# Loading the first quarter of w in two rounds through the same SBUF rows, and a different set of warm-up matmuls

## The chip, the cores and the metric

The kernel runs on one core of one Trainium2 chip. A core has a matrix engine (TensorE, PE in the profile, whose weight loads are listed apart as PEld), a vector engine (VectorE, DVE), a scalar engine (ScalarE, ACT), a general engine (GpSimd, POOL) and SyncE (SP), which only issues transfers here. SP and ACT issue loads whose type stays as it is (float32 to float32); POOL's loads convert float32 to bfloat16 on the way. The metric is the device time of one execution in microseconds. Before the change it is 904.03 us, the median of three runs (903.47 to 904.25).

## What is computed

x has 16 batches of 2048 time steps of 1024 values, w is 1024 by 1024, decay has one value for each of the 1024 output columns, all in float32. The reference is a matrix product followed by a running sum that decays:

```python
xw = x @ w
out[:, 0, :] = xw[:, 0, :]
for t in range(1, S):
    out[:, t, :] = decay[None, :] * out[:, t - 1, :] + xw[:, t, :]
```

## The kernel before

**The tiles.** Time is cut into chunks of 512 steps, 64 in all. For a chunk the kernel loads x as bfloat16 into a tile `xb`, turns it on DVE in 32 by 32 blocks into `xw` (the method `turn`, line 110), and copies it into `xt`, where the elements that lie in pairs are taken apart (the method `part`, line 119). The 1024 rows of w are the contraction. They are spread over the 128 partitions in four quads of 32 (q), and over 8 steps k; a step k = 2m + e has a row set m (0 to 3) and a parity e (0 or 1). A matmul (line 131) multiplies one step k of one block of 128 output columns n with up to 512 time steps, and eight of them add up in PSUM. Steps of parity 0 can read `xw` directly (argument `pairs`), those of parity 1 read `xt`. What follows the product (the scan along time on DVE, help from ACT and POOL, a turn back, the stores by SP) is not touched by the change.

**w.** The weights stay in SBUF as bfloat16 in `wsb`. They come in four quarters, named by a half of the columns h and a parity e. Quarter (0, 0) is loaded as float32 by SP and ACT, four loads of 256 KB (one for each quad, two on each engine), before anything else. The other three are loaded by POOL as bfloat16, four loads of 128 KB each. A quarter lies first in a staging area (`stage`, line 312), which borrows the room of output tiles, and is then copied into `wsb` by `settle` (line 324), one row set m at a time. For quarter (0, 0) that copy is also the cast from float32.

**The order.** Every instruction is pinned: each engine works off its own in the order in which the program writes them. For the start that order is a string, `agenda[-99]`, whose letters are functions of the table `deeds`, and whose numbers are their arguments:

- M0 to M3 load the halves of x's first two chunks, four loads of POOL each (one for each quad). The first chunk is cut into 320 and 192 time steps, the second into 256 and 256. U0 to U2 load w's quarters (0, 1), (1, 0) and (1, 1) by POOL.
- W and w settle one row set of w, W on DVE and w on ACT. Numbers 0 to 3 are quarter (0, 0), 4 to 7 quarter (0, 1).
- E turns one row set of one part of x on DVE. F (on DVE) and G (on ACT) do the copy into `xt`.
- K3 copies one value of x's quad 3 into a small tile `gate` (`spin_on`, line 355, on ACT), and then issues a matmul that uses `gate` as weights, so that TensorE stays in its place until x has come.
- R loads the decays by SP, D works on them.

Ahead of the agenda stand the loads of quarter (0, 0), three fills on DVE (`wide`, `seed`, `gate`), a copy on ACT from `wide` into `seed`, which brings ACT's table load with it, and `spin(5, seed, wide)`: five float32 matmuls of 512 columns, whose results are not used and whose weights `seed` wait for that copy. In the profile a float32 matmul appears as two records.

After the agenda TensorE starts the first chunk (line 653 on): for the first 320 time steps it takes the parity-0 steps k = 0, 2, 4, 6 with quarter (0, 0), four column blocks each, then k = 1, 3, 5, 7 with quarter (0, 1), and then the same for the other 192 time steps. The second chunk follows, in halves of 256.

Of the kernel before, what the change touches and what calls it, by code (L numbers as in the profile page):

```python
# [9 lines left out]
FP32 = mybir.dt.float32  # L10
BF16 = mybir.dt.bfloat16
# [3 lines left out]
def _ap(ap_obj: bass.AP, new_ap, extra_offset=0):  # L15
    return dataclasses.replace(
        ap_obj,
        ap=[list(p) for p in new_ap],
        offset=ap_obj.offset + extra_offset,
    )  # L20
# [5 lines left out]
def kernel(  # L26
# [26 lines left out]
    nc = tc.nc  # L53
    pin = tc.keep_in_program_order
    B, S, D = x.shape
    assert w.shape == (D, D)

    NQ = 4
    P = 32
    CQ = D // NQ  # L60
    K = CQ // P
    M = K // 2
# [3 lines left out]
    R = K // 2  # L66
    CH = D // 2
    CR = CH // NQ

    const = ctx.enter_context(tc.tile_pool(name="const", bufs=1))  # L70
# [9 lines left out]
    def quad(q):  # L80
        return slice(q * P, (q + 1) * P)
# [12 lines left out]
    def ot_tile(nj):  # L94
        return ring(sb, "ot", 4, [128, nj, CR])
# [14 lines left out]
    def turn(c, j0=0, j1=NJ, m0=0, m1=M):  # L110
        if c not in xw_of:
            xw_of[c] = ring(sb, "xw", 2, [128, M, NJ, P, 2], BF16)
        src = xb_of[c][:, j0:j1].rearrange("p j c -> p (j c)").bitcast(FP32)
        dst = xw_of[c].rearrange("p m j i e -> p (m j i e)").bitcast(FP32)
        pin(nc.vector.transpose(  # L115
            out=dst.rearrange("p (m j i) -> p j m i", m=M, i=P)[:, j0:j1, m0:m1],
            in_=src.rearrange("p (j m c) -> p j m c", m=M, c=P)[:, :, m0:m1]))
# [23 lines left out]
    class Tile:  # L141
# [45 lines left out]
        def copy(self):  # L187
            self.xs = sb.tile([128, 2 * TL], FP32, name=f"xs{self.lot % 3}")[:, 0:self.T]
            size = self.T // len(self.parts())
            for i, ps in enumerate(self.parts()):  # L190
                pin(nc.scalar.copy(out=self.xs[:, i * size:(i + 1) * size], in_=ps))  # L191
# [94 lines left out]
    class Outlet:  # L286
# [8 lines left out]
        def store(self, b, t0):  # L295
# [4 lines left out]
            for j in range(0, self.nj, nj):  # L300
# [8 lines left out]

    room = [ot_tile(2 * NJ).rearrange("p j c -> p (j c)") for _ in range(2)]  # L310
    size = M * CH
    stage = {(0, 0): room[0][:, 0:size],
             (0, 1): room[0][:, size:size * 3 // 2].bitcast(BF16),
             (1, 0): room[1][:, 0:size // 2].bitcast(BF16),
             (1, 1): room[1][:, size // 2:size].bitcast(BF16)}

    def load_w(queues, h, e):
        for i, q in enumerate((0, 2, 1, 3)):
            pin(queues[i % len(queues)].dma_start(  # L319
                out=stage[h, e][quad(q)].rearrange("p (m d) -> p m d", m=M),  # L320
                in_=_ap(w, [[2 * D, P], [2 * P * D, M], [1, CH]],
                        (q * CQ + e) * D + h * CH)))

    def settle(h, e, m, copy):
        src = stage[h, e][:, m * CH:(m + 1) * CH]
        pin(copy(out=wcols[:, 2 * m + e, h],  # L326
                 in_=src.rearrange("p (q r i) -> p q r i", q=NQ, r=R)))

    wide = const.tile([128, TL], FP32, name="wide")
    idle = wide[:, 0:TL // 2].bitcast(BF16)  # L330
    spare = ring(psp, "spare", 1, [128, TL])
    rows = const.tile([128, 2, P], FP32, name="rows")
    seed = const.tile([128, 128], FP32, name="seed")
    load_w((nc.sync, nc.scalar), 0, 0)
    pin(nc.vector.memset(wide, 0.0))
    pin(nc.vector.memset(seed, 0.0))
    pin(nc.scalar.copy(out=seed[:, 0:1], in_=wide[:, 0:1]))  # L337

    gate = const.tile([128, 128], BF16, name="gate")
    pin(nc.vector.memset(gate, 0.0))  # L340

    def spin(count, by, on):
        for _ in range(count):
            pin(nc.tensor.matmul(out=spare, lhsT=by, rhs=on, start=True, stop=True))  # L344

    spin(5, seed, wide)
    H = NJ // 2
    cuts = (((0, H + 2), (H + 2, NJ)), ((0, H), (H, NJ)))
    cols = const.tile([128, 2, P], FP32, name="cols")
# [8 lines left out]

    def load_part(i):
        load_w((nc.gpsimd,), *((0, 1), (1, 0), (1, 1))[i])  # L360

    def part_one(i, copy):
        part(i // 8, copy, i % 4, i % 4 + 1, *cuts[i // 8][i // 4 % 2])

    def settle_one(i, copy):
        settle(i // 8, i // 4 % 2, i % 4, copy)
# [119 lines left out]
    def turn_and_load(c):  # L486
# [16 lines left out]
        "w": lambda i: settle_one(i, nc.scalar.copy),  # L503
        "M": load_half,
        "U": load_part,
        "r": await_settled,
        "E": lambda i: turn(i // 8, *cuts[i // 8][i // 4 % 2], i % 4, i % 4 + 1),
        "F": lambda i: part_one(i, nc.vector.tensor_copy),
# [20 lines left out]
        "L": lambda i: load(*loads.pop(0)) if loads else None,  # L529
    }  # L530
    agenda = {
        -99: "M0 U0 M1 M2 M3 U1 U2 w0 W1 w2 W3 K3 E0 E1 G0 E2 G1 E3 F2 G3 W4 w5 W6 W7 E4 E5 G4 E6 G5 E7 F6 G7 R E8 E9 G8 E10 G9 E11 F10 G11 E12 L E13 G12 L E14 G13 E15 L F14 G15 D",
        0: "",
        1: "",
        2: "",
# [104 lines left out]
    for step, (g, n) in enumerate(slots):  # L640
# [11 lines left out]
        if step == 0:  # L652
# [9 lines left out]
            Q = cuts[1][0][1] * P  # L662
# [93 lines left out]
```

## Time and profile before

| what | value |
|---|---|
| median of three runs | 904.03 us (903.47 to 904.25) |
| the profiled execution's own time | 903.32 us |
| its span in the profile | 901.5 us |
| TensorE busy | 894.6 us, 99% |
| DVE, ACT, POOL busy | 825.8, 685.7, 656.8 us |
| moved by the transfers | 204.77 MB, mean 227 GB/s |
| first float32 matmul of the spins | 3.21 us |
| first settling of w | 7.04 us |
| x's first part turned from | 10.33 us |
| first matmul of the product | 10.90 us |

The times count from the start of the span. A line of the timeline gives the start, the duration, the engine, the line of the kernel, the operation, what it writes and reads, and in brackets how long the engine was idle just before it and what ended that. A line of the transfers' table gives a queue with its packets, megabytes and the share of 16 transfer engines' time; q0 is POOL's queue, q1 is SP's and q10 is ACT's. A line of the table of issues gives what is written and read, the issuing engine, the number of loads, the size of one and the median time from issue to landing.

### The profile page before, as it was taken

To read this page: it belongs to the slowest core of one execution; us is meant where nothing else is said; L and a number is where in the kernel's file an instruction comes from. 1 tells how busy PE (TensorE), PEld (TensorE's weight loads), DVE (VectorE), ACT (ScalarE), POOL (GpSimd) and SP (SyncE) were. 2 spreads that over 40 slices of the span, in tenths; PEclk is the share of its full clock that TensorE was granted. 3 is DMA by queue.
4 is the path that set the end of the run, shared out by engine and by line. 5 is a ranking of instruction groups with operands and counts; after the bars stand their busy time and mean duration, and the time that the engine had idled before them with its cause. 6 is when DMAs were issued, how large, how long until landed. Compare 5 with 4: busy or idle time off the path is not lost.

```text
span 901.5 us, 12309 instructions
## 1 busy us (share of the span) xinstructions
PE 894.6 (99%) x4211; PEld 412.8 (46%) x4211; DVE 825.8 (92%) x633; ACT 685.7 (76%) x957; POOL 656.8 (73%) x758
## 2 busy tenths in 40 slices
PE   8999999999999999999999999999999999999998
PEld 5544444444444444444444444444444444444444
DVE  4999989999999999999998999989999999999998
ACT  4888879877877877878778778777787787787743
POOL 7887778877767768677677687777777777776532
PEclk9999999999999999999999999999999999999999
DMA  9999999999999999999999999999999999999658
GB/s 189 192 211 244 244 205 215 215 230 240 248 237 264 242 254 242 256 253 246 220 245 218 228 241 211 239 223 228 236 228 223 229 235 226 230 219 219 187 135 239
DMA packets 403182, 204.77 MB, mean 227 GB/s; under 512 B 9392, under 2 KB 402096, under 8 KB 403120
## 3 DMA queue, kind: packets, MB, share of 16 engines
q0 software_dynamic: 137024, 68.70, 57.5%
q1 hardware_dynamic: 265808, 134.77, 57.1%
q8 instruction: 33, 0.54, 0.2%
q10 hardware_dynamic: 288, 0.52, 0.2%
q14 instruction: 29, 0.24, 0.1%
HBM read 138.42 MB, written 134.22 MB: 302 GB/s over the span
## 4 chain that ended last, share of the span: by engine, by line
PE 99%; ACT 0%; ACTq 0%; DVE 0%; DVEq 0%; issue 0%
PE ps L131 97%; PE spare L131 1%; PE spare L344 1%; ACT L337 0%; PE spare L412 0%; ACTq L319 0%; PE ps L412 0%; DVE h L440 0%; ACT seed L337 0%; DVEq L751 0%
## 5 line engine op out<-in xcount | busy, mean ns | idle before, releaser
L131 PE MATMUL ps<-xt,wsb 128*128 128x512 bf16 (+2 forms) x4040 | 865.9, 377 | 0.0
L131 PEld LDWEIGHTS <-wsb 128*128 128x128 bf16 x4184 | 408.3, 98 | 477.2 <-DVE wsb L326 0.3
L205 POOL TENSOR_TENSOR xs<-h,xs 128x512 f32<-128x512 f32 (+1 forms) x190 | 242.4, 1277 | 185.5 <-ACT h L171 84.4
L191 ACT COPY xs<-ps 128x1024 f32<-128x1024 f32 (+1 forms) x190 | 188.7, 994 | 153.4 <-PE ps L131 147.2
L278 DVE STREAM_TRANSPOSE ot<-so 128x1024 f32<-128x1024 f32 (+2 forms) x264 | 300.6, 1176 | 2.7 <-POOL so L266 2.0
L266 POOL TENSOR_TENSOR so<-h,xs 128x512 f32<-128x512 f32 (+1 forms) x189 | 240.6, 1274 | 38.4 <-ACT h L171 26.2
L123 ACT COPY xt<-xw 128x2048 bf16<-128x2048 bf16 (+3 forms) x136 | 242.4, 1788 | 5.8 <-DVE xw L115 5.8
L105 POOL DMA_DIRECT2D xb<-in_x_dram x264 | 173.8, 659 | 7.6 <-DMA xb<-in_x_dram 2.8
L171 ACT ACTIVATE h<-so,dec 128x512 f32<-128x512 f32 (+1 forms) x189 | 144.7, 766 | 26.6 <-DVE so L210 23.3
L115 DVE STREAM_TRANSPOSE xw<-xb 128x2048 f32<-128x2048 f32 (+3 forms) x78 | 147.2, 1899 | 6.1 <-DMA xb<-in_x_dram 6.1
L210 DVE TENSOR_TENSOR_SCAN so<-spare,keep,xs 128x512 f32<-128x512 f32 (+1 forms) x97 | 120.0, 1240 | 27.5 <-POOL xs L205 26.9
L210 DVE TENSOR_TENSOR_SCAN so<-spare,xs 128x512 f32<-128x512 f32 x93 | 113.3, 1220 | 25.9 <-POOL xs L205 22.6
L171 ACT ACTIVATE h<-ps,dec 128x512 f32<-128x512 f32 (+1 forms) x190 | 129.6, 683 | 0.0
L229 DVE TENSOR_TENSOR_SCAN so<-dec,ps 128x1024 f32<-128x1024 f32 x34 | 76.9, 2261 | 0.8 <-ACT h L171 0.6
L229 DVE TENSOR_TENSOR_SCAN so<-dec,keep,ps 128x1024 f32<-128x1024 f32 (+2 forms) x35 | 75.5, 2156 | 0.8 <-PE ps L131 0.8
L270 ACT COPY keep<-so 128x1 f32<-128x1 f32 x136 | 25.3, 188 | 9.3 <-DVE so L229 8.7
L201 ACT COPY so<-keep 128x1 f32<-128x1 f32 x97 | 18.3, 191 | 3.3 <-DVE ot L278 3.2
L199 POOL MEMSET so<- 128x1 f32 x93 | 10.6, 115 | 3.0 <-DVE ot L278 3.0
L131 PE MATMUL spare<-xt,wsb 128*128 128x512 bf16 (+3 forms) x60 | 12.6, 329 | 0.0
L131 PE MATMUL ps<-xw,wsb 128*128 128x256 bf16 (+3 forms) x72 | 12.2, 306 | 0.0
L344 PE MATMUL spare<-wide,seed 128*128 128x512 f32 x10 | 7.4, 915 | 3.2 <-ACT seed L337 3.2
L319 POOL DMA_DIRECT2D ot<-in_w_dram x12 | 6.5, 548 | 0.7 <-issue 0.3
(43 smaller groups left out, 37.6 us busy)
## 6 DMA issues: line engine op xcount, KB each, us to landing
out_dram<-ot SPq DMA_DIRECT2D x236, 512.0 KB, 8.9
xb<-in_x_dram POOLq DMA_DIRECT2D x248, 256.0 KB, 7.4
out_dram<-ot SPq DMA_DIRECT2D x56, 128.0 KB, 2.2
out_dram<-ot SPq DMA_DIRECT2D x8, 256.0 KB, 4.8
ot<-in_w_dram POOLq DMA_DIRECT2D x12, 128.0 KB, 5.8
xb<-in_x_dram POOLq DMA_DIRECT2D x8, 128.0 KB, 4.5
out_dram<-xb SPq DMA_DIRECT2D x3, 256.0 KB
xb<-in_x_dram POOLq DMA_DIRECT2D x4, 160.0 KB, 6.6
```

The lines of the kernel that those rows point to most:

```text
L105: pin(nc.gpsimd.dma_start(out=xb_of[c][quad(q), j0:j1], in_=_ap(x, [[D, P], [P * D, j1 - j0], [1, CQ]], (b * S + t0 + j0 * P) * D + q * CQ)))
L115: pin(nc.vector.transpose(out=dst.rearrange("p (m j i) -> p j m i", m=M, i=P)[:, j0:j1, m0:m1], in_=src.rearrange("p (j m c) -> p j m c", ...
L123: pin(copy(out=xt_of[c][:, m0:m1, :, j0 * P:j1 * P], in_=src))
L131: return pin(nc.tensor.matmul(out=ps[:, t0 % ps.shape[1]:][:, 0:t1 - t0], lhsT=lhs, rhs=rhs, start=(k == 0 and t0 == start), stop=(k == K ...
L171: pin(nc.scalar.activation(out=h[:, i * size:(i + 1) * size], in_=src, func=mybir.ActivationFunctionType.Copy, scale=dec[:, self.n:self.n ...
L191: pin(nc.scalar.copy(out=self.xs[:, i * size:(i + 1) * size], in_=ps))
L205: pin(nc.gpsimd.tensor_tensor(out=odds, in0=self.g, in1=odds, op=ALU.add))
L210: pin(nc.vector.tensor_tensor_scan(out=so[:, 3:T + 2:2], data0=squares[-1][:, n:n + 1].to_broadcast([128, T // 2]), data1=self.xs[:, 1:T:2 ...
L229: return pin(nc.vector.tensor_tensor_scan(out=so[:, t + 2:t + 2 + size], data0=dec[:, n:n + 1].to_broadcast([128, size]), data1=ps, initia ...
L266: pin(nc.gpsimd.tensor_tensor(out=self.so[:, 2:T + 2:2], in0=self.h, in1=self.xs[:, 0:T:2], op=ALU.add))
L270: pin(nc.scalar.copy(out=self.keep, in_=self.so[:, self.T + 1:self.T + 2]))
L278: pin(nc.vector.transpose(out=outlet.ot[:, :, c0:c0 + P], in_=self.so[:, 2 + t0:2 + t0 + nj * P].rearrange("p (i t) -> p i t", t=P)))
```

## The change

Quarter (0, 0) comes in two rounds, of row sets 0 and 1 and of row sets 2 and 3. Both go into the same rows of the staging area (`rounds`), so that the second round can be written only when both row sets of the first have been settled. Each round is four loads of 128 KB, two on SP and two on ACT; the second is the new deed Q. In the agenda, Q stands behind w0 and W1, and the settling of row sets 2 and 3 (w2 on ACT, W3 on DVE) moves behind gates and turns of x. There is one more gate, K2, for x's quad 2. The turns E0 to E3 stand ahead of the copies G0, G1, F2, G3, and w2 and W3 among them.

The spins become four float32 matmuls that read `wide` for the weights as well, and so wait for its fill and no longer for ACT's copy, and two bfloat16 matmuls with `gate`. `seed` shrinks to one column and loses its fill; ACT's copy into it stays.

```diff
-    stage = {(0, 0): room[0][:, 0:size],
-             (0, 1): room[0][:, size:size * 3 // 2].bitcast(BF16),
+    early = M // 2
+    rounds = room[0][:, 0:early * CH]
+    stage = {(0, 1): room[0][:, size:size * 3 // 2].bitcast(BF16),
...
-    def load_w(queues, h, e):
+    def staged(h, e, m0, m1):
+        if (h, e) == (0, 0):
+            return rounds[:, m0 % early * CH:][:, 0:(m1 - m0) * CH]
+        return stage[h, e][:, m0 * CH:m1 * CH]
+
+    def load_w(queues, h, e, m0=0, m1=M):
         for i, q in enumerate((0, 2, 1, 3)):
             pin(queues[i % len(queues)].dma_start(
-                out=stage[h, e][quad(q)].rearrange("p (m d) -> p m d", m=M),
-                in_=_ap(w, [[2 * D, P], [2 * P * D, M], [1, CH]],
-                        (q * CQ + e) * D + h * CH)))
+                out=staged(h, e, m0, m1)[quad(q)].rearrange("p (m d) -> p m d", m=m1 - m0),
+                in_=_ap(w, [[2 * D, P], [2 * P * D, m1 - m0], [1, CH]],
+                        (q * CQ + e + 2 * P * m0) * D + h * CH)))
 
     def settle(h, e, m, copy):
-        src = stage[h, e][:, m * CH:(m + 1) * CH]
         pin(copy(out=wcols[:, 2 * m + e, h],
-                 in_=src.rearrange("p (q r i) -> p q r i", q=NQ, r=R)))
+                 in_=staged(h, e, m, m + 1).rearrange("p (q r i) -> p q r i", q=NQ, r=R)))
...
-    seed = const.tile([128, 128], FP32, name="seed")
-    load_w((nc.sync, nc.scalar), 0, 0)
+    seed = const.tile([128, 1], FP32, name="seed")
+    load_w((nc.sync, nc.scalar), 0, 0, 0, early)
     pin(nc.vector.memset(wide, 0.0))
-    pin(nc.vector.memset(seed, 0.0))
-    pin(nc.scalar.copy(out=seed[:, 0:1], in_=wide[:, 0:1]))
+    pin(nc.scalar.copy(out=seed, in_=wide[:, 0:1]))
...
-    spin(5, seed, wide)
+    spin(4, wide[:, 0:128], wide)
+    spin(2, gate, idle)
...
+    def load_rest(i):
+        load_w((nc.sync, nc.scalar), 0, 0, early, M)
...
+        "Q": load_rest,
...
-        -99: "M0 U0 M1 M2 M3 U1 U2 w0 W1 w2 W3 K3 E0 E1 G0 E2 G1 E3 F2 G3 W4 w5 W6 W7 E4 E5 ...
+        -99: "M0 U0 M1 M2 M3 U1 U2 w0 W1 Q K2 K3 E0 E1 w2 E2 E3 W3 G0 G1 F2 G3 W4 w5 W6 W7 E4 E5 ...
```

## The prediction, made before the changed kernel was run

> **What bounds the kernel now.** I read the page's busy table and chain first, to see which engine sets the end.
>
> ```profile
> span 901.5 us, 12309 instructions
> PE 894.6 (99%) x4211; PEld 412.8 (46%) x4211; DVE 825.8 (92%) x633; ACT 685.7 (76%) x957; POOL 656.8 (73%) x758
> PE 99%; ACT 0%; ACTq 0%; DVE 0%; DVEq 0%; issue 0%
> ```
>
> TensorE is the chain. From its first real matmul at 10.90 us it has no idle time until the last microseconds, so whatever moves its first tile moves the end by as much. The change touches only the stretch before 20 us; I went through it in order of time.
>
> ```profile
> 3.21 7.42 PE L344 MATMUL spare<-wide,seed 128*128 128x512 f32 x10 [3.21 <-ACT seed L337]
> 7.04 1.14 ACT L326 CAST wsb<-ot 128x512 bf16<-128x512 f32 x2 [3.87 <-DMA ot<-in_w_dram]
> 7.07 0.76 DVE L326 CAST wsb<-ot 128x512 bf16<-128x512 f32 x2 [5.45 <-DMA ot<-in_w_dram]
> 10.29 0.19 ACT L356 COPY gate<-xb 32x1 bf16<-32x1 bf16 x1 [2.11 <-DMA xb<-in_x_dram]
> 10.33 1.69 DVE L115 STREAM_TRANSPOSE xw<-xb 128x320 f32<-128x320 f32 x4 [2.50 <-DMA xb<-in_x_dram]
> 10.88 1.98 ACT L123 COPY xt<-xw 128x640 bf16<-128x640 bf16 x3 [0.40 <-DVE xw L115]
> 12.92 0.62 ACT L326 COPY wsb<-ot 128x512 bf16<-128x512 bf16 x1
> 12.94 0.70 DVE L326 COPY wsb<-ot 128x512 bf16<-128x512 bf16 x3 [0.54 <-DMA ot<-in_w_dram]
> 15.00 1.16 DVE L115 STREAM_TRANSPOSE xw<-xb 128x192 f32<-128x192 f32 x4 [1.36 <-DMA xb<-in_x_dram]
> 17.71 1.42 DVE L115 STREAM_TRANSPOSE xw<-xb 128x256 f32<-128x256 f32 x4 [1.24 <-DMA xb<-in_x_dram]
> 20.42 1.42 DVE L115 STREAM_TRANSPOSE xw<-xb 128x256 f32<-128x256 f32 x4 [0.98 <-DMA xb<-in_x_dram]
> ```
>
> w's first quarter lies in SBUF at 7.0, the first part of x at 10.3, the second quarter (POOL's first w loads) at 12.9, the rest of x's first chunk at 15.0, the next chunk's halves at 17.7 and 20.4. TensorE turns to each at 10.90, 13.29, 15.48, 18.21 and 21.77. The first four come 0.3 to 0.6 us after the data, a transpose or copy and no more: TensorE and the transfers run level here.
>
> Last the transfers, in three windows: 0 to 5.4, 16.5 to 20.0 and 20.0 to 21.4 us.
>
> ```profile
> q1 hardware_dynamic: 275, 0.51, 41.5%
> q10 hardware_dynamic: 227, 0.43, 20.7%
> xb<-in_x_dram POOLq DMA_DIRECT2D x4, 160.0 KB, 6.6
> ot<-in_w_dram POOLq DMA_DIRECT2D x3, 128.0 KB, 7.2
> ```
>
> ```profile
> q0 software_dynamic: 1350, 0.68, 143.4%
> rows<-in_decay_dram SPq DMA_DIRECT2D x4, 1.0 KB
> ```
>
> ```profile
> q0 software_dynamic: 304, 0.28, 121.3%
> q1 hardware_dynamic: 48, 0.00, 4.9%
> ```
>
> Up to 5.4 us POOL had issued seven loads and its queue moved nothing: w's 1 MB stood in front. From 16.50 SP had four tiny loads out, and up to 20.0 only POOL's queue moved. Loads are served roughly in the order in which they came.
>
> **The change, part by part.**
>
> *First round.* Half the bytes: 0.52 MB on SP and ACT, two loads each. Before, the first load of each queue carried those bytes and landed 4.0 and 4.2 us after issue, at 4.9. m=0 is then cast on ACT (0.62 each in the groups) and m=1 on DVE (0.42): done at 5.55.
>
> *x.* It stood behind 1.05 MB and now behind 0.52. The float32 queues moved 322 GB/s between 3 and 5 us, so 1.6 us less: landed at 8.6 instead of 10.2, first real matmul about 9.25. Two k steps of four matmuls (steps start 0.56 us apart in the timeline, so 1.1) use the two settled sets and end at 10.4. That gain is real, but only if the next weights are there.
>
> *Spins.* They now wait for the memset (ended 1.40) and not for ACT's copy (ended 3.16), so they start 1.8 us sooner; each float32 spin is two records, 0.855 us apart cold. Four end by 1.45 + 8 x 0.855 = 8.3, the two bf16 by 9.2 at worst. The new gate on x's third quarter adds an ACT copy (0.19) and a spin (0.39). The dropped memset (0.17) was off the path. All this costs nothing: it ends before TensorE's new idle time, which is its cover; without that cover it would be 0.6 us.
>
> *Second round.* It goes into the same rows, so SP and ACT wait for both casts: issued at 5.6 and 6.05 (an issue takes 0.4). ACT then idles anyway; the decay loads behind it on SP are not due until 16.5. By 5.6 POOL has issued eight loads (1.31 to 5.42): x's four and w's second quarter. When does this round land? Lower bound: SP's undisturbed 128 KB stores land 2.2 us after issue, so 8.3. Upper bound: behind all eight. The eighth, issued at 5.42, landed 7.4 us later, at 12.8, less 1.6 for the bytes no longer ahead, 11.2; plus 0.52 MB at 322 GB/s, 1.6: 12.8. Nearest is the decay load: issued at 16.50, its first packets moved after 20.0, when POOL's load of 15.48 (1.0 before) landed, but that of 16.04 (0.5 before) landed only at 21.1. So an SP load goes behind POOL loads issued a full microsecond earlier. The last pair at 6.05 goes behind seven, the eighth (5.42) is undecided: 12.8, or 12.8 less its 0.65 (131 KB at 200 GB/s), 12.15. I take 12.4.
>
> *What queues behind it.* The order written for ACT is: cast m=2, three copies of x, then the second quarter's m=1. From the rows: 12.4 + 0.1 + 0.57 + 1.98 + 0.62 = 15.67. TensorE takes m=2 at 13.1 and m=3 after it (DVE's cast is done at 12.9), then the second quarter's first step, and waits for that last copy: three steps remain, 15.67 + 0.12 + 3 x 0.556 = 17.46. In the profile this point is 15.48. DVE's chain (0.42 + 0.45 + 0.29) is shorter, and the second quarter itself is in by 12.8, since the same bytes have moved. So TensorE is **1.98 us later**. The next data (15.0, 17.7, 20.4) now wait for TensorE with over 2 us to spare, so nothing gives the time back or adds to it.
>
> *Sum.* The profiled execution takes 903.32 (span 901.5 and 1.8 around it): 905.3. The median of the three runs is 0.71 above it, 904.03: **906.0**. With landings of 12.15 and 12.8 it is 905.8 and 906.4; if two POOL loads are overtaken (11.5), 905.1.
>
> **The rivals.** Of this kernel, 0.2% (1.8 us) is about what a measurement can tell from no change.
>
> *Clock.* TensorE idles from 10.4 to 13.1, 2.7 us, after its warm-up. The float32 weight loads stand 0.855 us apart up to 8.49 and 0.43 apart at the end: it needs some 5.7 us of work to reach full rate. If the pause loses that, up to 5.7 us run at half rate, 2.85 us lost, of which 0.9 hides in the wait for ACT's copy: 1.9 more, 907.9. Against it: the granted clock is 1.00 in every row, and no pause of that length is in the trace. It decides if the second round lands later than about 13.
> The Trainium skill (TensorE: Matmul & The Clock Gate, Why this matters for your kernels) advises against idle gaps over about 3 us between bursts, after which the array drops to half rate; by that this pause just escapes. No run here shows such a drop yet.
>
> *Hidden.* The engines could alternate between queues. From 128 to 130 us POOL's queue moved 427 packets and SP's 432, which speaks for it; the empty windows above speak against it while POOL has many loads out. Then the second round lands by about 10, is settled before it is due, and the second quarter, for which the same bytes have passed, arrives at 12.9 as before: nothing to 0.3 us gained, 903.9.
> The Trainium skill (DMA: Bandwidth & Descriptors, Queues, rings and completion order) says that each DMA engine goes round robin between its queues by packets; by that this rival is the forecast. The window from 16.5 to 20.0 disagrees: 1350 packets to none.
>
> *Faster.* If float32 traffic rides beside POOL's at no cost: the one moved 322 GB/s alone, the other 200. Then 0.52 MB (1.6 us) vanish from ahead of everything after, and POOL's slow stretch (161 and 137 GB/s at 6 to 8 us) mends up to 0.5: each arrival and TensorE 2.1 us earlier, 901.9. It decides once the second round lands before 9.5 and the 17.71 arrival comes before 16. Against it: at 128 to 130 both together moved 214 GB/s, hardly more than POOL's queue alone.
>
> *Not as said:* the first round lands no sooner than 7. Half its bytes make this negligible.
>
> **How the numbers follow.** Late second round 64%: 905.1 to 906.4 by the landing, and 0.4 either way by the median; I put 0.38 above the 0.2% bound (905.8) and 0.26 under it. Clock 14%, all slower. Hidden 13%, within. Faster 9%. So slower 0.38 + 0.14 = 0.52, same 0.26 + 0.13 = 0.39, faster 0.09. The range 903.0 to 908.2 leaves out the last rival and the worst of the clock's.
>
> **What would show it.** First cast at about 4.9; x's gate near 8.6; ACT's and DVE's second casts released by the w load at 12.2 to 12.9; a TensorE idle time of 2 to 3 us before the third step, then about 1 us before the second quarter's second set; the first chunk's second part starting near 17.5. Second casts before 10.5 would prove the forecast wrong, and so would the 17.7 arrival moving by more than 1 us, either way. Float32 or real matmuls at double spacing after the pause mean the clock.

## The result and the profile after

The changed kernel takes 906.62 us (median of eight runs, 905.93 to 907.47), the kernel before 903.54 us beside it (903.33 to 904.49). The ratio is 1.0032, with a 95% interval of 1.0021 to 1.0043: slower by 3.1 us. The forecast was 906.0 (903.0 to 908.2), slower with a chance of 0.52. The profiled execution took 907.19 us with a span of 905.4, against 903.32 and 901.5.

TensorE and the other engines in the timeline of the changed kernel, from the first cast to the second chunk:

```profile
5.07 0.62 ACT L331 CAST wsb<-ot 128x512 bf16<-128x512 f32 x1 [1.91 <-DMA ot<-in_w_dram]
9.76 1.69 DVE L115 STREAM_TRANSPOSE xw<-xb 128x320 f32<-128x320 f32 x4 [4.22 <-DMA xb<-in_x_dram]
10.33 0.59 PE L131 MATMUL ps<-xw,wsb 128*128 128x320 bf16 x3
11.32 0.30 PE L131 MATMUL spare<-xw,wsb 128*128 128x320 bf16 x1
...
13.40 0.62 ACT L331 CAST wsb<-ot 128x512 bf16<-128x512 f32 x1 [3.50 <-DMA ot<-in_w_dram]
13.44 0.43 DVE L331 CAST wsb<-ot 128x512 bf16<-128x512 f32 x1 [1.98 <-DMA ot<-in_w_dram]
13.93 1.97 ACT L123 COPY xt<-xw 128x640 bf16<-128x640 bf16 x3
14.07 0.67 PE L131 MATMUL ps<-xw,wsb 128*128 128x320 bf16 x3 [2.45 <-ACT wsb L331]
...
15.78 1.16 DVE L115 STREAM_TRANSPOSE xw<-xb 128x192 f32<-128x192 f32 x4 [0.85 <-DMA xb<-in_x_dram]
15.81 0.61 ACT L331 COPY wsb<-ot 128x512 bf16<-128x512 bf16 x1
...
19.03 0.42 PE L131 MATMUL ps<-xw,wsb 128*128 128x192 bf16 x3
...
21.73 0.84 PE L131 MATMUL ps<-xw,wsb 128*128 128x256 bf16 x6
```

The first round is there at 5.0, as meant, and the product starts at 10.33 instead of 10.90. Then TensorE stands still from 11.6 to 14.07, until the second round has landed and ACT has cast it (from 13.40 on). The lead of 0.57 us becomes a lag of 3.5: the first chunk's second part starts at 19.03 instead of 15.48, the second chunk at 21.73 instead of 18.21. After that the lag stays: the first copy out of PSUM starts at 26.40 instead of 22.88, and the last store is issued at 902.05 instead of 898.52, 3.5 us later each time. The span ends 3.9 us later; the 0.4 us behind the last store's issue (3.35 us to the end of the span, 2.98 before) are not explained here.

The queues of the changed kernel in two windows, 5.7 to 9.2 and 9.2 to 12.5 us (packets, megabytes, share), with the issues of the first:

```profile
q0 software_dynamic: 936, 0.53, 118.9%
...
ot<-in_w_dram SPq DMA_DIRECT2D x2, 128.0 KB, 6.6
ot<-in_w_dram ACTq DMA_DIRECT2D x2, 128.0 KB, 6.7
```

```profile
q0 software_dynamic: 428, 0.37, 70.4%
q1 hardware_dynamic: 159, 0.26, 24.2%
q10 hardware_dynamic: 158, 0.26, 21.5%
```

SP and ACT issued the second round at 5.7 and 6.1. Up to 9.2 only POOL's queue moved anything; then the three queues moved side by side. The four loads took 6.6 and 6.7 us to land.

And the granted clock (the third number from the end of each line) in three stretches of the changed kernel:

```profile
12.00:14.00 2.00, 0.00 (x0) 0.00 (x0) 0.56 (x2) 0.60 (x2) 1.37 (x2) 1.00 1.39 198
14.40:16.00 1.60, 1.60 (x8) 0.91 (x7) 0.75 (x4) 1.60 (x4) 1.60 (x4) 0.52 1.45 193
16.00:17.80 1.80, 1.80 (x9) 0.96 (x8) 1.26 (x6) 1.66 (x4) 1.80 (x4) 0.50 1.46 190
```

No matmul runs from 12 to 14 us, and soon after the pause the clock is at half. The matmuls of 320 columns then start 0.27 us apart and not 0.14, until 17.7. Not in every run: four of the eight have a mean granted clock of 0.997 or 0.998 over the whole span and took 906.9 to 907.5; the other four have 0.999 or 1.000 and took 905.9 to 906.3.

### The profile page after: what moved, and what is told of

It reads as the page before. It is cut to its first block, busy times and chain, and to the rows that moved or that the text cites. A ratio compares the mean times of both kernels' runs of the same rounds, so it can differ in the third digit from the quotient of the medians.

```text
span 905.4 us, 12242 instructions
## 1 busy us (share of the span) xinstructions
PE 892.3 (99%) x4131; PEld 413.4 (46%) x4212; DVE 824.8 (91%) x632; ACT 685.1 (76%) x958; POOL 657.5 (73%) x758
## 4 chain that ended last, share of the span: by engine, by line
PE 98%; DMA 1%; issue 1%; ACT 0%; ACTq 0%; DVE 0%; DVEq 0%
PE ps L131 96%; PE spare L131 1%; DMA ot<-in_w_dram 1%; ACT wsb L331 0%; PE spare L420 0%; ACTq L325 0%; PE ps L420 0%; DVE h L448 0%; DVEq L760 0%; ACTq L331 0%
## 5 line engine op out<-in xcount | busy, mean ns | idle before, releaser
L131 PE MATMUL ps<-xt,wsb 128*128 128x512 bf16 (+1 forms) x3959 | 862.5, 377 | 4.3
L131 PE MATMUL ps<-xw,wsb 128*128 128x256 bf16 (+3 forms) x72 | 12.8, 314 | 2.5 <-ACT wsb L331 2.5
L131 PE MATMUL spare<-xt,wsb 128*128 128x512 bf16 (+3 forms) x60 | 12.8, 333 | 0.0
L348 PE MATMUL spare<-wide 128*128 128x512 f32 x8 | 6.7, 1023 | 1.5 <-DVE wide L340 1.5
```

What stands on the lines that cost most here:

```text
L131: return pin(nc.tensor.matmul(out=ps[:, t0 % ps.shape[1]:][:, 0:t1 - t0], lhsT=lhs, rhs=rhs, start=(k == 0 and t0 == start), stop=(k == K ...
```

## The experiments

The theory: the second round stands behind what POOL has already out, TensorE waits for it, and the wait brings two more costs, ACT's row of work and the clock. The rivals: the spins, the new order of the work, or a landing that has nothing to do with POOL's loads. All ratios are to the kernel before, run on the same chip in the same session (903.37 us for the spins alone, the rows of their own, the second quarter held back and the pause filled; 903.43 for the other three). The intervals are some 0.2% wide, 2 us, so a difference of a few tenths between two of these kernels is read from the traces, not from the medians alone.

### The spins alone

```diff
# kernel before
-    spin(5, seed, wide)
+    spin(4, wide[:, 0:128], wide)
+    spin(2, gate, idle)
```

(`seed` as in the change.)

> Theory (late second round): the spins are not the cause. The kernel before with the change's spins starts the product within 0.2 us of 10.90 and takes 903.3 to 903.8 us. Rival (spins): warm-up that starts and ends sooner leaves the array at half rate when the product starts; then at least 1 us of the 3.1 us shows, 904.5 us or more, with a granted clock under 1.00 between 10 and 15 us.

Measured: 903.62 us (903.17 to 905.00, 11 runs), ratio 1.0008 (0.9999 to 1.0017). In the profiled execution the product starts at 10.79, clock 1.00. So the spins don't explain the 3.1 us. But the rival has a grain of truth. Six runs lie at 903.2 to 903.6 and five at 904.7 to 905.0; four of these five have a mean clock of 0.997 or 0.998, none of the six. The fifth has 1.000, and three of the 23 runs of the kernel before lie at 904.3 to 904.5 with clocks of 0.999 and 1.000, so a run can be a microsecond longer for another reason, which is open. The warm-up now ends at 7.5, and the gate's matmul comes at 10.44:

```profile
10.44 0.39 PE L343 MATMUL spare<-wide,gate 128*128 128x512 bf16 x1 [2.90 <-ACT gate L356]
```

The profiled execution itself kept its clock through this pause of 2.9 us. The four runs with the lower clock are about 1.4 us longer than the six; that they lost it over this pause is inferred, as they have no trace.

### The order and the spins, but one round

```diff
# changed kernel
-    rounds = room[0][:, 0:early * CH]
+    rounds = room[0][:, 0:size]
-            return rounds[:, m0 % early * CH:][:, 0:(m1 - m0) * CH]
+            return rounds[:, m0 * CH:][:, 0:(m1 - m0) * CH]
-    load_w((nc.sync, nc.scalar), 0, 0, 0, early)
+    load_w((nc.sync, nc.scalar), 0, 0)
-        -99: "... w0 W1 Q K2 K3 ...
+        -99: "... w0 W1 K2 K3 ...
```

> The changed kernel with the whole first quarter in one round of four 256 KB loads, as before; spins, second gate, and the order of casts, turns and copies stay. Theory (the two rounds alone cost the time): x's first part lands at 10.2 us, the product starts at 10.9, no pause over 0.5 us, granted clock 1.00; 903.3 to 904.4 us, since the cast of the third set now stands behind the gates on ACT and may cost 0.3. Rival (the new order costs it): 905 us or more.

Measured: 903.75 us (903.17 to 905.33, 11 runs), ratio 1.0004 (0.9995 to 1.0012), product from 10.90, no pause in it. The longest pause lies ahead of it, after the warm-up:

```profile
9.89 0.39 PE L348 MATMUL spare<-wide,gate 128*128 128x512 bf16 x1 [2.09 <-ACT gate L361]
```

The two longest of the eleven runs (904.61 and 905.33) are the two with a mean clock of 0.998. With spins, second gate and order all in place, only the way in which the first quarter is loaded makes the difference. The two rounds are the cause; whether by the shared rows or by the smaller loads, this run doesn't tell.

### Rows of their own, issued at once

This one was meant to show the same, and did not. It is called own_rows further on.

```diff
# changed kernel; rows of their own as above, and:
     load_w((nc.sync, nc.scalar), 0, 0, 0, early)
+    load_w((nc.sync, nc.scalar), 0, 0, early, M)
-        -99: "... w0 W1 Q K2 K3 ...
+        -99: "... w0 W1 K2 K3 ...
```

> The changed kernel with rows of their own for the second round, issued right behind the first, ahead of everything on SP and ACT; spins, second gate and order stay. Theory (late second round): it lands with 0.5 us of the 6.9 us of before, no pause after the second step, granted clock 1.00, and the time is that of before, 903.2 to 904.2 us. Rival (order of the turns, casts and gates, or the spins): the pause goes, but 1 us or more of the 3.1 us stays, 904.6 us or more.

Measured: 906.37 us (905.55 to 907.56, five runs), ratio 1.0034 (1.0022 to 1.0047), as slow as the change. Against the theory as I had put it, and it is not the order either, as the run with one round shows. The trace shows another cause: x came late. DVE's first turn and what it waited for:

```profile
11.86 1.69 DVE L115 STREAM_TRANSPOSE xw<-xb 128x320 f32<-128x320 f32 x4 [5.83 <-DMA xb<-in_x_dram]
```

11.86 instead of 10.33. The gate's matmul came 4.5 us after the warm-up, and the clock was at 0.50 from 12 to 14; four of the five runs have a mean clock of 0.996 to 0.998. Rows of their own are no cure: the same eight loads lost as much in another way, so what sharing the rows costs by itself is not separated. The new theory was that eight loads of 128 KB are not the same as four of 256, so I tried them alone.

### Eight loads in the kernel before

```diff
# kernel before; load_w takes m0 and m1 as in the change, each set keeps its own rows
-    load_w((nc.sync, nc.scalar), 0, 0)
+    load_w((nc.sync, nc.scalar), 0, 0, 0, M // 2)
+    load_w((nc.sync, nc.scalar), 0, 0, M // 2, M)
```

> The kernel before with the first quarter in eight loads of 128 KB instead of four of 256 KB, sets 0 and 1 first, rows, order and spins as before. own_rows, which did this too, came out no faster than the change, against the theory. Theory now (the later loads of SP and ACT, issued at 1.7 to 2.1 us, come in between POOL's first loads, and the queues then move less): x's first part lands at 11.2 to 11.9 us instead of 10.2, the second quarter near 14, and the time is 904.4 to 906.0 us. Rival (own_rows was slow by its order of work and its pause alone): x's first part at 10.0 to 10.5 and 903.2 to 904.0 us.

Measured: 905.63 us (903.63 to 906.53, ten runs), ratio 1.0021 (1.0011 to 1.0030). In the profiled execution, one of the shorter ones (904.35), x is turned from 11.06, the second quarter is copied from 13.64. The stretch from 4 to 6 us in the kernel before, in this one, and with rows of their own (the last number is GB/s):

```profile
4.00:6.00 2.00, 2.00 (x4) 0.74 (x3) 0.00 (x0) 0.00 (x0) 1.96 (x4) 1.00 0.98 295
```

```profile
4.00:6.00 2.00, 1.83 (x2) 0.84 (x3) 0.36 (x1) 0.51 (x2) 2.00 (x4) 1.00 0.78 162
```

```profile
4.00:6.00 2.00, 2.00 (x5) 0.90 (x4) 0.40 (x1) 0.56 (x2) 2.00 (x4) 1.00 0.73 137
```

With the first quarter split, the transfers move about half in this stretch. From 6 to 8 us they make up for most of it (248 GB/s with eight loads, 149 in the kernel before), so that from 2 to 8 us 1.31 MB moved and not 1.38. The first turn was a little earlier than forecast (11.06 against 11.2 to 11.9), the time within. The loads' rows are as long as before; what differs is that four loads of SP and ACT are issued at 1.7 to 2.1 us and not by 1.2, after POOL's first. The queues do mix: from 4 to 5 us POOL's moved 55 packets beside 75 of SP's and ACT's, in the kernel before none beside 143. Whether this or the number of loads makes the transfers slower was not separated. The trace accounts for 0.7 us, by which the product starts later (11.63); the other 1.5 us of the median are in runs without a trace, and not by the clock, which is 0.999 or 1.000 in all ten. The warm-up also starts a microsecond later here (4.17), as ACT has two more issues ahead of its copy.

### The second quarter held back

If the second round waits for what POOL has out, it must land sooner when POOL has less out.

```diff
# changed kernel: POOL reads the two settled sets (r0, r1) before it issues the second quarter (U0)
-        -99: "M0 U0 M1 M2 M3 U1 U2 w0 W1 Q K2 K3 ...
+        -99: "M0 w0 W1 Q r0 r1 U0 M1 M2 M3 U1 U2 K2 K3 ...
```

> The changed kernel with POOL held, by two small copies that read the settled sets, until the first round is settled; only then it issues the second quarter's four loads, so that the second round stands behind x's four loads alone. Theory (served in order of arrival): the second round lands by 10.7 to 11.6 instead of 13.3 us, the pause falls under 1 us, the second quarter lands at about 13.5, and the time falls to 904.0 to 905.0 us. Rival (the landing does not depend on what POOL has out): the second round still lands after 12.8 us, and the time is 906.2 us or more.

Measured: 904.50 us (904.07 to 905.31, 11 runs), ratio 1.0013 (1.0004 to 1.0022): about two thirds of the loss are gone.

```profile
11.18 0.62 ACT L331 CAST wsb<-ot 128x512 bf16<-128x512 f32 x1 [2.10 <-DMA ot<-in_w_dram]
11.70 1.97 ACT L123 COPY xt<-xw 128x640 bf16<-128x640 bf16 x3
11.85 0.60 PE L131 MATMUL ps<-xw,wsb 128*128 128x320 bf16 x3 [1.08 <-ACT wsb L331]
13.35 0.70 DVE L331 COPY wsb<-ot 128x512 bf16<-128x512 bf16 x3 [1.31 <-DMA ot<-in_w_dram]
13.70 0.58 PE L131 MATMUL ps<-xt,wsb 128*128 128x320 bf16 x3 [0.55 <-ACT xt L123]
```

The second round's cast moves from 13.40 to 11.18, though the round was issued only 0.16 us sooner than in the change. The pause shrinks to 1.1 us, and no run shows a clock under 0.999. The second quarter now comes at 13.35 and not at 12.94 as in the kernel before: what one load gains in the row of transfers, the next one loses. TensorE's second wait, 0.55 us, ends with two things at once: ACT's last copy of x, done at 13.67, and the first copy of the second quarter, done at 13.64. So neither alone would have removed it. The product started at 9.48 here, 1.4 us sooner than in the kernel before, and the kernel still takes 1.1 us longer.

### The pause filled

This kernel is called fill_pause further on.

```diff
# changed kernel, in the first chunk's loop
                     for k in range(e, K, 2):
+                        if (j0, k) == (0, 4):
+                            for _ in range(11):
+                                pin(nc.tensor.matmul(out=spares[1], lhsT=gate, rhs=idle, start=True, stop=True))
```

> The changed kernel with eleven bf16 matmuls of 512 columns on an idle PSUM bank between the second and the third step (2.4 us of work whose results are not used). Theory (the pause also costs the clock): granted clock 1.00 from 10 to 20 us, matmuls of 320 columns 0.14 us apart after the pause, then a short wait for the copy of the second quarter's second set (about 16.5 us), the first chunk's second part at 18.2 instead of 19.0; 905.6 to 906.1 us, and the runs closer together. Rival (the clock is not what cost it, ACT's order alone): 906.4 us or more.

Measured: 906.07 us (905.96 to 906.56, seven runs), ratio 1.0029 (1.0017 to 1.0040). The clock is 1.00 in all four windows from 10 to 18 us, and no run's mean is under 0.999; the seven runs lie within 0.6 us, where the change's eight spread over 1.5. The first chunk's second part starts at 17.82 and not 19.03. Of these 1.2 us, 0.3 are an earlier landing in this run (third step from 13.78, not 14.07). From the third step to the second part it is 4.04 us and not 4.96, so the clock costs 0.9 us where it drops. The change's own runs agree: the four with the drop average 907.1, the four without 906.1. In the medians 0.4 of it is left (2.70 us above the kernel before, not 3.08), as it drops in half the runs; that difference alone would not be clear of noise. At full clock another wait shows, for the copy that ACT gets to last:

```profile
15.51 0.61 ACT L331 COPY wsb<-ot 128x512 bf16<-128x512 bf16 x1
16.18 0.58 PE L131 MATMUL ps<-xt,wsb 128*128 128x320 bf16 x3 [0.55 <-ACT wsb L331]
```

### That copy on DVE

```diff
# kernel with the pause filled
-        -99: "... F2 G3 W4 w5 W6 W7 ...
+        -99: "... F2 G3 W4 W5 W6 W7 ...
```

> fill_pause with one letter changed: the second quarter's second set is copied by DVE and not by ACT, so that it no longer stands behind ACT's cast and three copies. Theory (ACT's order costs 0.55 us once the clock is kept up): no wait ahead of that step, first chunk's second part at 17.3 instead of 17.8, and 905.4 to 905.7 us. Rival (the second quarter's landing or DVE's own row of copies ends that wait as late): within 0.2 us of fill_pause's 906.07.

Measured: 905.39 us (905.00 to 907.00, ten runs), ratio 1.0023 (1.0014 to 1.0033). No wait is left ahead of that step, and the first chunk's second part starts at 17.39, 3.31 us behind the third step and not 4.04: it gains 0.7 us on the kernel with the pause filled, in the trace as in the medians (1.96 us above the kernel before, not 2.70). What remains is the late third step, which starts at 14.08, against 12.02 in the kernel before. Not all of that is the landing:

```profile
11.71 2.54 PE L670 MATMUL spare<-wide,gate 128*128 128x512 bf16 x11
13.04 0.62 ACT L331 CAST wsb<-ot 128x512 bf16<-128x512 f32 x1 [2.89 <-DMA ot<-in_w_dram]
14.08 0.59 PE L131 MATMUL ps<-xw,wsb 128*128 128x320 bf16 x3
```

The cast was done at 13.66, and the third step starts 0.4 us after it, where the eleven matmuls that fill the pause come to their end. This execution is the second longest of the ten (905.86); how much the fill adds to the others is not known, so 1.96 is a little too much for the landing alone. None of the seven kernels beats the kernel before.

## Why the prediction was right, and where it was not

**The sign and the mechanism hold, and the size was too small.** The forecast put 1.98 us on top of 904.03; measured are 3.08 on top of 903.54. That 906.0 is only 0.6 off 906.62 is in part luck: the median of three runs that it started from was 0.5 too high, which hid almost half of what the sum lacked. By medians, each against the kernel before of its session, the change loses 3.08, with the pause filled 2.70, with the copy on DVE as well 1.96. That is 0.38 for the clock, 0.74 for ACT's row of work and 1.96 for the late third step, the fill's share in it included. The traces say 0.9 for the clock in an execution that loses it, 0.7 for ACT's row, and 2.05 for the third step of the change (14.07 against 12.02). The forecast had the landing and ACT's row as one sum of 1.98, and the clock as a rival of its own. The Trainium skill (DMA: Bandwidth & Descriptors, Queues, rings and completion order) lets each DMA engine take the queues in turn by packets; the window of 936 packets to none disagrees for the first 3.5 us, and the window behind it (428 to 159 and 158) agrees, once the loads' turn has come.

**First round:** forecast 4.9, measured 5.07 for the first cast. Issue of the second: forecast 5.6 and 6.05, measured 5.7 and 6.1. Right.

**x:** forecast 8.6, measured 9.7. This term was mis-sized. I gave x the 1.6 us that half of w's bytes take at 322 GB/s. But once the first round was in, POOL's queue was alone and moved 151 GB/s from 4 to 6 us and 136 from 6 to 8, not the 200 it reaches later. The error did not matter for the first matmuls, which had to wait anyway. It did for what follows.

**Landing of the second round:** forecast 12.4, with 12.8 as the last bound; ACT's cast began at 13.40, so it was in by 13.3. The bound failed for the same reason: it had POOL's eight loads through 1.6 us sooner than before, at 11.2, and then this round. But the eighth, issued at 5.66, landed 8.0 us later, at 13.7, where it had been 12.8 in the kernel before. The place in the row was right in part: the round stood behind x's four loads, but with the second quarter's it took turns from 9.2 us on, and was in before the last of them.

**The pause:** forecast 2.7 us, measured 2.45 idle and 2.75 between two starts.

**What queues behind:** forecast a wait of about 1 us for the copy on ACT. With the clock kept up TensorE is idle for 0.55 in the trace, and the copy on DVE gains 0.7. In the change itself it can't be seen: at half clock TensorE gets there after the copy.

**The clock:** put at 14%, it came in four runs of eight. Its price was forecast at 1.9 us on top; 0.9 was measured, since the half-rate stretch was 3.4 us long and not 5.7 (1.7 us lost), and the wait for ACT's copy hid part. The 5.7 was one execution's value: the warm-up's weight loads begin at 1.46 and stand 0.855 us apart up to 7.60 in the change, but only up to 4.18 with rows of their own. Nor does a granted clock of 1.00 tell all: the column shows 1.00 from 4 to 6 us in the kernel before, where the warm-up still runs at this wide spacing. I had let the clock decide once the round lands later than about 13, and 13.3 was past that. The Trainium skill (TensorE: Matmul & The Clock Gate, Why this matters for your kernels) puts the limit at gaps of over about 3 us; here kernels with gaps of 1.55 to 2.9 us lost the clock in some runs and kept it in others, and the one with gaps of up to 1.1 never did.

**Later arrivals:** forecast unmoved and covered. They came 0.8 to 1.0 us later (15.78, 18.52 and 21.40 for DVE's turns), and were covered: no wait of TensorE for them is in the trace.

**The rivals:** Hidden and Faster both needed the second round by 10. It came 3 us too late for either. What Hidden started from, that the queues move side by side, did hold from 9.2 us on, too late to help.

## What to carry to other kernels

A load that starts only when its buffer is free joins the end of a row that other engines have filled meanwhile; ask what is out at its issue, not how fast its queue is. Where transfers and the matrix engine run level, bringing one piece forward only pays if the later pieces move too: with the second quarter held back the product started 1.4 us sooner and the kernel was still slower. A pause of 2 or 3 us on the matrix engine can be dearer than its length, since in some runs the clock was halved after it (for 3.4 us in the one traced here), so judge such a change by many runs. And take the time before the change from as many runs as the time after it.

## What I had not expected of the hardware

Splitting four loads of 256 KB into eight of 128 KB, with the same rows and bytes and nothing waiting, cost 2.2 us (905.63 against 903.43) and left runs 2.9 us apart. In the trace of one of the shorter runs the queues mix earlier, x comes 0.7 us later, and the rest is open.

The clock went with the length of a pause, but not at one limit. By the longest pause of TensorE in each kernel's profiled execution, from the end of the warm-up on, the runs with a mean clock of 0.998 or less are none of 11 at 1.1 us (the quarter held back), one of 10 at 1.55 (the copy on DVE), two of 11 at 2.1 (one round), four of 8 at 2.45 (the change), four of 11 at 2.9 (the spins alone) and four of 5 at 4.5 (rows of their own). Such runs are about 1.0 us longer than the others with the change, and about 1.4 with the spins alone. Runs without a trace may have had other pauses than the profiled one, so this is a trend and not a rule.
